# Batch norm behind a matmul: another form and place for the fourth tile's normalisation, denser column chunks, later outputs of the fifth tile

## Chip, cores, metric

One core of a Trainium2 chip. The metric is the device time of one execution in microseconds (us). A run of this one-core kernel counts as slow when it is over 1.5% above the fastest of the same kernel; ratios use the other runs.

## The reference

```python
batch, m, k, n = 16, 512, 1024, 768
y = np.matmul(x, weight)                       # (16, 512, 768), M = 8192 rows
mean = np.mean(y, axis=(0, 1), keepdims=True)
var = np.var(y, axis=(0, 1), keepdims=True)
return (gamma * (y - mean) / np.sqrt(var + eps) + beta).astype(np.float32)
```

The statistics go over all rows, so no output can be stored before its column's last matmul.

## The kernel before

The 768 columns are six tiles of 128. The first three are computed while x is loaded, then their statistics are closed, and their outputs leave as *row products* (VectorE multiplies, L283; GpSimd adds the shift, L289) or, for 4 of the 16 chunks of 512 rows, as *column chunks* (normalise, transpose on TensorE, copy on ScalarE, store). Meanwhile TensorE computes the fourth, fifth and sixth tile. Their outputs leave in *pairs* of chunks: two normalisations, eight transposes, one copy of 1.0 us, one store of 512 KB. The sixth tile's go singly at the end, 16 stores of 256 KB. A schedule written in model times (`at(t, ...)`) is sorted and fixes each engine's order.

```python
def norm(nt, c, eng):
    if eng == "act":
        seq(nc.scalar.activation(y(nt, c), y(nt, c), AF.Identity,
            bias=shift[:, nt:nt + 1], scale=scale[:, nt:nt + 1]))
    else:
        seq((nc.vector if eng == "dve" else nc.gpsimd).tensor_scalar(
            y(nt, c), y(nt, c), scale[:, nt:nt + 1], shift[:, nt:nt + 1],
            op0=ALU.mult, op1=ALU.add))
# ... cut ...
def outputs(nt, t0, step):
    for b in range(C // 2):                    # pairs of chunks
        tb = t0 + step * b
        if nt == NT - 2 and b >= C // 2 - HELD:
            held.append(b)                     # the fifth tile's last pair waits for the end
            continue
        for i in range(2):
            at(tb - 2.2 + 0.5 * i, norm, nt, 2 * b + i, "act" if tb < tr + 2.0 and i == 0 else "dve")
        at(tb, turn_y, (nt,), 2 * b * CH, 2 * RT)
        at(tb + 2.2, out_copy, (nt,), 2 * b * CH, "act")
        at(tb + 2.3, store, (nt,), 2 * b * CH, 2 * RT)
# ... cut: the matmuls of tiles 3 to 5; pe is the model time at which a tile's matmuls end ...
    if nt == GA:
        outputs(nt, S + 37.0, 2.3)             # fourth tile
    elif nt < NT - 1:
        outputs(nt, pe + 4.6, 1.85)            # fifth tile
    else:
        held_outputs(nt - 1, pe)
        last_outputs(nt, pe + 3.0)             # sixth tile
```

The transposes stand between the matmuls, one after each, until they run out. A transpose that waits for its normalisation holds up all matmuls behind it.

## Time and profile before

| | before |
|---|---|
| time | 219.95 us, median of 3 (219.61 to 220.23); 219.41 over 6 runs later |
| span of the profiled run | 217.6 us |
| busy: TensorE, VectorE, ScalarE, GpSimd | 92%, 72%, 56%, 62% |
| first store | 136 us |

The span is read as four terms that add up: the start of the column sums (L232, when the loading stage is over; it scatters by up to 2 us between profiles), from there to the first half-chunk matmul (L330, the sixth tile's last chunk), from there to the last DMA byte, and a rest. I call the second the *matmul phase* and the third the *tail*. TensorE's timeline of the kernel before has the two marks:

```profile
123.21 1.39 PE L232 MATMUL tot_ps<-ones,sum 128*128 128x1 f32 x12
197.38 1.98 PE L330 MATMUL y_ps<-xT_sb,w_sb 128*128 128x256 bf16 x16
```

The last DMA byte is worked out from stretches of 2 us: in the last one that moved data, its GB/s over 346, the rate of a full DMA here, tell how far into it the transfer reached. Before: matmul phase 74.2, tail 18.6 (197.4 to 216.0).

### The profile page before, as it was taken

How to read it: one execution, taken by the hardware profiler on the slowest of the kernel's cores; microseconds unless marked ns; L12 is line 12 of the kernel's file. 1: busy time of each engine (PE TensorE's matmuls, PEld its weight loads, DVE VectorE, ACT ScalarE, POOL GpSimd, SP SyncE). 2: the span in 40 equal slices, each digit the busy share in tenths (PEclk: the TensorE clock that was granted, in tenths of full speed). 3: DMA queues.
4: the chain of work that ended last, by engine and by line, in shares of the span. 5: the costliest groups of instructions: out<-in, count | busy, mean ns of one | idle time of the engine just before them, and what ended most of it. 6: DMA issues, size and time to landing. Idle time of an engine off the chain costs nothing.

```text
span 217.6 us, 3451 instructions
## 1 busy us (share of the span) xinstructions
PE 200.3 (92%) x1178; PEld 104.9 (48%) x1178; DVE 155.8 (72%) x263; ACT 121.2 (56%) x227; POOL 134.2 (62%) x153
## 2 busy tenths in 40 slices
PE   7997999999999999999999999999999979997900
PEld 2452555554544565645656545444444435554600
DVE  3222978887978789998654369988899999728900
ACT  2001463645543466645666414967866689976950
POOL 8887686878684699953558304999995963000000
PEclk9999999999999999999999999999999999999985
DMA  5999999999999999993000000897877989999998
GB/s 70 156 196 187 191 196 196 197 197 196 196 189 195 197 196 196 196 197 49 0 5 0 0 0 0 305 348 293 304 286 293 332 274 370 338 347 284 282 345 243
DMA packets 70161, 43.75 MB, mean 201 GB/s; under 512 B 4096, under 2 KB 69632, under 8 KB 70144
## 3 DMA queue, kind: packets, MB, share of 16 engines
q0 software_dynamic: 34624, 18.36, 61.6%
q1 hardware_dynamic: 35520, 25.18, 35.8%
q8 instruction: 9, 0.15, 0.3%
q14 instruction: 8, 0.07, 0.1%
HBM read 36.71 MB, written 25.17 MB: 284 GB/s over the span
## 4 chain that ended last, share of the span: by engine, by line
PE 75%; DVE 8%; DMA 5%; POOL 3%; issue 3%; ACT 2%; ACTq 1%; POOLq 0%
PE y_ps L196 39%; PE y_ps L186 29%; PE o_ps L398 5%; DMA w_sb<-in_weight_dram 3%; DMA ring<-in_x_dram 2%; DVE stats L316 2%; DVE y_sb L382 2%; DVE ring L283 2%; POOL w_sb L149 2%; DVE o_sb L283 1%; ACT o_sb L411 1%; POOL ring L162 1%; PE y_ps L330 1%; PE a_ps L272 1%; PE tot_ps L232 1%
## 5 line engine op out<-in xcount | busy, mean ns | idle before, releaser
L196 PE MATMUL y_ps<-xT_sb,w_sb 128*128 128x512 bf16 (+1 forms) x484 | 117.6, 381 | 1.6 <-DMA w_sb<-in_weight_dram 1.3
L196 PEld LDWEIGHTS <-w_sb 128*128 128x128 bf16 x484 | 45.9, 96 | 59.3 <-issue 3.1
L343 ACT CAST y_sb<-y_ps 128x512 bf16<-128x512 f32 x59 | 34.5, 585 | 53.7 <-DVE stats L316 50.7
L186 PE MATMUL y_ps<-w_sb,xT_sb 128*128 128x384 bf16 x384 | 63.4, 326 | 0.0
L316 DVE BATCH_NORM_STATS2 stats<-y_ps 128x6 f32<-128x512 f32 x58 | 39.3, 685 | 19.9 <-PE y_ps L196 19.9
L162 POOL DMA_DIRECT2D ring<-in_x_dram x72 | 45.2, 633 | 11.9 <-DVE xT_sb L174 6.5
L186 PEld LDWEIGHTS <-xT_sb 128*128 128x128 bf16 x384 | 37.5, 98 | 25.6
L212 POOL TENSOR_TENSOR sum<-sum,sq_sb 128x384 f32<-128x384 f32 x38 | 38.0, 1001 | 18.4 <-ACT sq_sb L208 17.1
L174 DVE STREAM_TRANSPOSE xT_sb<-ring 128x1024 f32<-128x1024 f32 (+1 forms) x34 | 39.5, 1168 | 12.8 <-DMA ring<-in_x_dram 12.8
L398 PE MATMUL o_ps<-ident,y_sb 128*128 128x128 bf16 x240 | 38.2, 219 | 3.6 <-DVE y_sb L382 2.5
L289 POOL TENSOR_TENSOR ring<-ring,sum 128x768 f32<-128x768 f32 x17 | 31.1, 1864 | 13.1 <-ACT sum L274 12.1
L215 DVE TENSOR_TENSOR sum<-y_ps,sum 128x384 f32<-128x384 f32 x48 | 26.1, 544 | 14.4 <-ACT sq_sb L208 13.4
L208 ACT ACTIVATE sq_sb<-y_ps 128x384 f32<-128x384 f32 x48 | 23.4, 492 | 15.2 <-PE y_ps L186 11.6
L221 ACT CAST y_sb<-y_ps 128x384 bf16<-128x384 f32 x48 | 22.9, 476 | 7.3 <-DVE sum L215 7.0
L411 ACT CAST ring<-o_ps 128x1024 f32<-128x1024 bf16 (+1 forms) x24 | 22.5, 951 | 4.2 <-PE o_ps L398 2.7
L398 PEld LDWEIGHTS <-y_sb 128*128 128x128 bf16 x240 | 19.4, 97 | 8.6 <-DVE y_sb L382 3.3
L382 DVE TENSOR_SCALAR y_sb<-y_sb,scale,shift 128x512 bf16<-128x512 bf16 x43 | 22.0, 565 | 0.0
L283 DVE TENSOR_TENSOR ring<-y_sb,a_ps 128x768 f32<-128x768 bf16 x17 | 15.9, 937 | 0.0
L289 POOL TENSOR_TENSOR o_sb<-o_sb,sum 128x768 f32<-128x768 f32 x7 | 13.2, 1880 | 2.9 <-DVE o_sb L283 2.9
L377 ACT ACTIVATE y_sb<-y_sb,shift,scale 128x512 bf16<-128x512 bf16 x17 | 13.5, 816 | 0.0
L155 PE MATMUL idle_ps<-idle_sb 128*128 128x512 bf16 x38 | 11.0, 456 | 1.2 <-DVE idle_sb L103 1.2
L411 ACT CAST o_sb<-o_ps 128x512 f32<-128x512 bf16 x16 | 7.9, 679 | 0.3 <-PE o_ps L398 0.3
(62 smaller groups left out, 50.1 us busy)
## 6 DMA issues: line engine op xcount, KB each, us to landing
ring<-in_x_dram POOLq DMA_DIRECT2D x56, 256.0 KB, 8.6
out_dram<-ring SPq DMA_DIRECT2D x25, 384.0 KB, 3.0
out_dram<-ring SPq DMA_DIRECT2D x16, 512.0 KB, 5.1
out_dram<-o_sb SPq DMA_DIRECT2D x16, 256.0 KB, 3.7
out_dram<-o_sb SPq DMA_DIRECT2D x7, 384.0 KB, 3.4
ring<-in_x_dram POOLq DMA_DIRECT2D x16, 128.0 KB, 5.3
w_sb<-in_weight_dram POOLq DMA_DIRECT2D x8, 96.0 KB, 4.6
w_sb<-in_weight_dram POOLq DMA_DIRECT2D x4, 192.0 KB, 5.6
```

Source lines behind the costliest of these rows:

```text
L162: seq(nc.gpsimd.dma_start(x_bf[32 * i:32 * i + 32], src[:, :, KQ * i:KQ * (i + 1)]))
L174: seq(nc.vector.transpose(dst[:, half, :, jw0:jw1], src[:, :, jw0:jw1]))
L186: seq(nc.tensor.matmul(y_ps, xT[c][:, jw, s * P:(s + 1) * P, e], w_sb[:, jw, e, 0:NA], start=(jw == 0 and e == 0), stop=(jw == JW - 1 and ...
L196: seq(nc.tensor.matmul(y_ps, w_sb[:, jw, e, nt * P:(nt + 1) * P], xT[c][:, jw, q0 * QR:q1 * QR, e], start=(jw == 0 and e == 0 and q0 == 0) ...
L212: seq(eng.tensor_add(acc, acc, py.pop(("sq", c, s))))
L215: seq(nc.vector.tensor_add(sum1, py["row", c, s][:, 0:NA], sum1))
L289: seq(nc.gpsimd.tensor_add(o_sb, o_sb, sum1[:, None, :].to_broadcast([P, 2, NA])))
L316: seq(nc.vector.bn_stats(stats_of(nt)[:, i, :], py[nt, c]))
L343: seq(nc.scalar.copy(y(nt, c), py.pop((nt, c))))
L382: seq((nc.vector if eng == "dve" else nc.gpsimd).tensor_scalar(y(nt, c), y(nt, c), scale[:, nt:nt + 1], shift[:, nt:nt + 1], op0=ALU.mult, ...
L398: seq(nc.tensor.transpose(dst, src, ident))
L411: seq(nc.scalar.copy(o_sb, src))
```

## The change

Its aim, as far as its words and code tell: keep VectorE from waiting for GpSimd. The fourth tile's VectorE normalisations get a form without a fast mode, more of them go to ScalarE, pairs come less often, and the fifth tile's start after the crowd.

```diff
+        elif eng == "dve1":
+            seq(nc.vector.scalar_tensor_tensor(
+                y(nt, c), y(nt, c), scale[:, nt:nt + 1],
+                shift[:, nt:nt + 1].to_broadcast([P, CH]), op0=ALU.mult, op1=ALU.add,
+            ))
@@ column chunks
-            tk += 9.6 if c else 7.2
+            tk += 8.2 if c else 7.2
@@ outputs()
-                at(tb - 2.2 + 0.5 * i, norm, nt, 2 * b + i, "act" if tb < tr + 2.0 and i == 0 else "dve")
+                at(tb - (2.8 if tb < tr else 2.2) + 0.5 * i, norm, nt, 2 * b + i,
+                   "dve" if tb > tr + 2.0 else "dve1" if i and b % 2 == 0 else "act")
@@ starts and steps
-            outputs(nt, S + 37.0, 2.3)
+            outputs(nt, S + 36.0, 2.8)
-            outputs(nt, pe + 4.6, 1.85)
+            outputs(nt, pe + 10.5, 2.3)
```

## The prediction

> **What bounds the kernel now.** I read the page first: the 40 slices, then the chain that ended last.
>
> ```profile
> PE   7997999999999999999999999999999979997900
> DVE  3222978887978789998654369988899999728900
> DMA  5999999999999999993000000897877989999998
> PE 75%; DVE 8%; DMA 5%; POOL 3%; issue 3%; ACT 2%; ACTq 1%; POOLq 0%
> ```
>
> TensorE is busy to slice 37; the output DMA is full in the last ten slices or so. The chain in order of time says where TensorE is not the bound: it runs on TensorE from 19.3 to 156.9 us, on VectorE to about 178.7 us, on TensorE again to 199.4 us (the last statistics), then through the last tile's outputs to the end. So two stretches matter: 157 to 179 us, and the tail. VectorE's timeline in the first:
>
> ```profile
> 161.26 3.38 DVE L382 TENSOR_SCALAR y_sb<-y_sb,scale,shift 128x512 bf16<-128x512 bf16 x1
> 166.03 1.62 DVE L382 TENSOR_SCALAR y_sb<-y_sb,scale,shift 128x512 bf16<-128x512 bf16 x1
> 173.80 0.45 DVE L382 TENSOR_SCALAR y_sb<-y_sb,scale,shift 128x512 bf16<-128x512 bf16 x1
> ```
>
> The same form has a median of 0.41 us over its 43 calls. GpSimd's timeline explains the excess:
>
> ```profile
> 160.86 1.84 POOL L289 TENSOR_TENSOR o_sb<-o_sb,sum 128x768 f32<-128x768 f32 x1
> 162.65 1.84 POOL L289 TENSOR_TENSOR ring<-ring,sum 128x768 f32<-128x768 f32 x1
> 165.67 1.83 POOL L289 TENSOR_TENSOR o_sb<-o_sb,sum 128x768 f32<-128x768 f32 x1 [1.18 <-DVE o_sb L283]
> 172.22 1.88 POOL L289 TENSOR_TENSOR ring<-ring,sum 128x768 f32<-128x768 f32 x1
> ```
>
> Each normalisation ends 0.15 us after a GpSimd addition ends (164.64 after 164.49, 167.65 after 167.50, 174.25 after 174.10). The first waited out two additions, because the second was already ready when it asked; the others waited only for the running one. What reaches TensorE of this is small:
>
> ```profile
> 167.71 0.23 PE L398 MATMUL o_ps<-ident,y_sb 128*128 128x128 bf16 x1 [0.30 <-DVE y_sb L382]
> 170.64 0.23 PE L398 MATMUL o_ps<-ident,y_sb 128*128 128x128 bf16 x1 [0.50 <-DVE y_sb L382]
> 175.32 0.23 PE L398 MATMUL o_ps<-ident,y_sb 128*128 128x128 bf16 x1 [0.23 <-ACT y_sb L377]
> 178.69 0.23 PE L398 MATMUL o_ps<-ident,y_sb 128*128 128x128 bf16 x1 [0.94 <-ACT y_sb L377]
> ```
>
> From start to start, beside the usual 0.28 us, these four lose 0.41, 0.61, 0.34 and 1.05: 2.4 us. That is all that can be won there. The tail, in stretches of 2 us (the last two columns are the DMA's share and GB/s):
>
> ```profile
> 198.00:200.00 2.00, 1.80 (x20) 1.43 (x18) 1.30 (x4) 0.96 (x2) 0.00 (x0) 1.00 1.15 343
> 200.00:202.00 2.00, 0.53 (x8) 0.44 (x8) 1.73 (x9) 1.57 (x4) 0.00 (x0) 1.00 0.20 59
> 202.00:204.00 2.00, 2.00 (x28) 1.37 (x25) 2.00 (x8) 2.00 (x5) 0.00 (x0) 1.00 0.96 292
> 204.00:206.00 2.00, 2.00 (x28) 1.37 (x26) 2.00 (x7) 2.00 (x5) 0.00 (x0) 1.00 1.15 347
> ```
>
> The DMA has emptied its queue at about 200.2, idles 2 us, starts again at about 202.3 and then runs at 346 GB/s to 216.0: one held store of 512 KB and sixteen of 256 KB, 4.72 MB, 13.6 us. The end of the span is 1.6 us later. Before the gap the fifth tile's stores have kept it full since 186.
>
> **What the Trainium skill says.** (1) "SBUF — State Buffer", section "SBUF: two separate sides": VectorE and GpSimd share one pair of ports, as an exclusive lock for a whole instruction; a VectorE operation takes it in a two-port mode or with two SBUF inputs (then only against a GpSimd operation that reads SBUF). The waits above agree for the two-port mode. For two inputs the earlier stage has two cases, L212, an addition of two SBUF tensors that normally takes 0.55 us:
>
> ```profile
> 89.43 0.77 DVE L212 TENSOR_TENSOR sum<-sum,sq_sb 128x384 f32<-128x384 f32 x1
> 94.81 1.10 DVE L212 TENSOR_TENSOR sum<-sum,sq_sb 128x384 f32<-128x384 f32 x1
> ```
>
> GpSimd's triples that started at 86.62 and 92.32 end at 89.79 and 95.50; these two end at 90.20 and 95.91, both 0.41 us later. They waited too. (2) "VectorE: DVE Perf Modes", section "The perf-mode tier table": `tensor_scalar` in bf16 reaches four elements a cycle, a two-tensor operation with an fp32 operand one. The trace agrees: 0.41 us for 512 elements above, 0.55 us for 384 in L212.
>
> **The change, part by part.**
> (a) *Fourth tile.* Before: nine normalisations in the fast form on VectorE, seven on ScalarE. The built order of the changed kernel has nine on ScalarE, three of the new form (the second chunk of pairs 0, 2 and 4), four fast ones for pairs 6 and 7 (a pair is two chunks that are stored together). The new form reads y and a broadcast fp32 shift, two SBUF inputs. Free, I estimate 0.68 us: L283's 768 elements take 0.94, L212's 384 take 0.55, so 512 lie at 0.68. So it is 0.27 us dearer, and if it locks, it waits like the old one and ends 0.54 us after GpSimd, not 0.15.
> (b) *Working it through with the lock*, with the durations above, in the new order: the first one asks at 159.8, waits for the running addition and a ready one, to 162.7, and ends at 163.2. The second asks at 167.7, gets in at 169.65, ends at 170.2. The third asks at 174.0, ends at 175.3. Behind it stand the last statistics (0.69), a row product (0.94) and the aggregate (0.57), so the aggregate is done at 177.3, against 176.2 before. ScalarE then has, in order, the square root, a cast, three small affine steps, a copy of 1.0 and only then pair 5's first normalisation: 180.3. TensorE wants it at 177.7. Stalls: 0.2 for pair 1, 0.6 for pair 2 (ScalarE behind casts that wait for VectorE), 0.1, then 2.6 and 0.1: 3.6 us in place of 2.4.
> (c) *Fifth tile later.* The order of TensorE's instructions shows 72 transposes behind the last matmul before, 92 after: 20 fewer in the matmul stream. There a transpose adds 0.056 us (0.282 against 0.226 a step), so the last matmul comes 1.1 us sooner. The 20 fit into TensorE's idle 2 us while the last statistics are finished.
> (d) *The tail.* Those 20 belong to half of pair 4 and to pairs 5 and 6, so three stores of 512 KB move behind the last matmul, 1.5 us of DMA each. Pair 4's copy on ScalarE cannot start until its last four transposes, 0.35 us after the last matmul (199.4 in the old times); copy 1.0; 0.95 from its end until the DMA flows, as with the held store before: 201.7. From there 4 x 512 KB + 16 x 256 KB = 6.29 MB at 346 GB/s are 18.2 us, ending at 219.9 against 216.0: **+3.9 us**, less what the last matmul is earlier. The DMA's spare time meanwhile lies at 187 to 200, where stores of 1.5 us come every 2.3 us.
> (e) *Denser column chunks* bring twelve transposes ahead of the VectorE-bound stretch and change no count.
> Sum: +3.9 (d), -1.1 (c), +1.2 (b) = +4.0 with the lock, so about 224; without the lock and without stalls, 3.9 - 1.1 - 2.4 = +0.4, so 220.3.
>
> **The rivals.**
> *Plain mode is free of the lock.* Then VectorE takes back some 6 us and all stalls go: 220.3. For it: the change seems made with that in mind, and the second operand has step zero, which no run here has tried. Against: the two L212 cases and the skill's page.
> *TensorE's gain passes whole to the end*, the tail being hidden: 2.4 + 1.1 us won, 216.5. Against: the tail has 18.2 us of transfer behind one copy that comes after the last matmul; the order of the instructions fixes that. I see no way round it.
> *The stalls grow*: ScalarE, in order, carries two more normalisations and waits on VectorE in between; one more wait for a ready addition (1.84 us) makes 226.
>
> **Range and chances.** The tail's +3.9 I hold for firm within 0.5; the stalls are uncertain by 1.5 us, as I may have a request on the wrong side of a GpSimd addition, and slips more often loosen than tighten this sum. I give the lock 70%. That puts the middle at 222.6, between 220.3 and 224. Slower by over 2% needs 224.35, which the lock case reaches in a fifth to a quarter of its outcomes: 0.15. Faster by 2% needs 215.6, below even the rival with everything won: 0.02.
>
> **What would show it.** Lock: the three new operations last 1.4 to 3.5 us each and end about 0.54 after a GpSimd addition; at 0.7 they are free of it. Stalls: TensorE's waits at its transposes in 160 to 181 us add up to over 2 us and the largest is on ScalarE near 178; under 1 us proves (b) wrong. Tail: DMA share below 0.9 between 187 and 199, full for about 18 us at the end, and last matmul to last DMA byte 20.5 us instead of 16.6. If the last distance stays at 17, (d) is wrong; then I am too high by 3 us.

## The result

222.38 us (median of 6, 221.34 to 223.07) against 219.41 (6 runs): ratio 1.0133, 95% interval 1.0089 to 1.0177, which is "same" at 2%; the interval lies above 1, so the changed kernel is slower, by 0.9 to 1.8%. The span of the profiled run is 220.6 us. The page of the changed kernel, the same rows as shown of before:

```profile
PE   7997999999999999999999999999999979997400
DVE  3222878887978789998554289988999995588300
DMA  5999999999999999990000001996995999888997
PE 71%; DMA 9%; DVE 8%; ACT 5%; issue 2%; POOL 1%; ACTq 0%; POOLq 0%
```

In the 40 slices the DMA row is the one to look at: before, its last nine slices read 989999998, now 999888997, and the chain has 9% of DMA instead of 5%. TensorE's marks:

```profile
123.45 1.39 PE L232 MATMUL tot_ps<-ones,sum 128*128 128x1 f32 x12
196.23 1.98 PE L330 MATMUL y_ps<-xT_sb,w_sb 128*128 128x256 bf16 x16
```

The matmul phase is 72.8, **1.4 us shorter** than before. Yet the end is later. The tail in stretches of 2 us (last two columns: DMA share, GB/s), first the last stretch of the kernel before, then the changed kernel:

```profile
214.00:216.00 2.00, 0.00 (x0) 0.00 (x0) 0.00 (x0) 0.00 (x0) 0.00 (x0) 0.50 1.13 339
```

```profile
188.00:190.00 2.00, 2.00 (x22) 1.22 (x20) 0.64 (x2) 1.89 (x3) 0.00 (x0) 1.00 0.32 96
196.00:198.00 2.00, 2.00 (x20) 1.61 (x18) 1.97 (x7) 1.44 (x3) 0.00 (x0) 1.00 0.72 217
198.00:200.00 2.00, 1.77 (x30) 1.58 (x28) 1.16 (x5) 1.49 (x4) 0.00 (x0) 1.00 0.53 157
200.00:202.00 2.00, 0.98 (x13) 0.69 (x14) 1.91 (x8) 2.00 (x4) 0.00 (x0) 1.00 0.85 254
218.00:220.00 2.00, 0.00 (x0) 0.00 (x0) 0.00 (x0) 0.00 (x0) 0.00 (x0) 0.50 0.42 125
```

The DMA idles where it was full before (345 GB/s at 188, 348 at 196) and is full from about 200.5 on to 218.7 (218 + 2 x 125/346; before, 214 + 2 x 339/346 = 216.0). The tail is 22.5 us instead of 18.6: **+3.9**. With +0.2 for the start of the column sums and +0.3 for the rest behind the last byte, +0.2 - 1.4 + 3.9 + 0.3 = +3.0, the difference of the two spans.

The new form on VectorE:

```profile
160.03 3.46 DVE L383 SCALAR_TENSOR_TENSOR y_sb<-y_sb,scale,shift 128x512 bf16<-128x512 bf16 x1
167.81 0.80 DVE L383 SCALAR_TENSOR_TENSOR y_sb<-y_sb,scale,shift 128x512 bf16<-128x512 bf16 x1
172.32 2.10 DVE L383 SCALAR_TENSOR_TENSOR y_sb<-y_sb,scale,shift 128x512 bf16<-128x512 bf16 x1
```

and GpSimd's additions beside it:

```profile
161.09 1.85 POOL L289 TENSOR_TENSOR o_sb<-o_sb,sum 128x768 f32<-128x768 f32 x1
...
166.22 1.83 POOL L289 TENSOR_TENSOR o_sb<-o_sb,sum 128x768 f32<-128x768 f32 x1
168.02 2.27 POOL L289 TENSOR_TENSOR ring<-ring,sum 128x768 f32<-128x768 f32 x1
...
173.84 2.27 POOL L289 TENSOR_TENSOR o_sb<-o_sb,sum 128x768 f32<-128x768 f32 x1
```

All three end 0.55 us after an addition ends (163.49 after 162.94, 168.61 after 168.05, 174.42 after 173.87): they wait like the fast form did. Where VectorE went first, the next addition lasts 2.27 instead of 1.83, so GpSimd waits too. TensorE's waits at its transposes:

```profile
169.15 0.23 PE L404 MATMUL o_ps<-ident,y_sb 128*128 128x128 bf16 x1 [0.37 <-ACT y_sb L377]
179.50 0.23 PE L404 MATMUL o_ps<-ident,y_sb 128*128 128x128 bf16 x1 [1.63 <-ACT y_sb L377]
```

Two stalls, 2.0 us of idle time, as much as the four before. The larger is the predicted one: pair 5's first normalisation on ScalarE, behind the aggregate and what ScalarE does with it.

### The profile page after: what moved, and what is told of

It is laid out like the page before. It is cut to its first block, busy times and chain, and to the rows that moved or that the text cites. A ratio compares the mean times of both kernels' runs of the same rounds, so it can differ in the third digit from the quotient of the medians.

```text
span 220.6 us, 3437 instructions
## 1 busy us (share of the span) xinstructions
PE 199.3 (90%) x1163; PEld 105.2 (48%) x1178; DVE 154.9 (70%) x262; ACT 121.2 (55%) x228; POOL 134.7 (61%) x153
## 4 chain that ended last, share of the span: by engine, by line
PE 71%; DMA 9%; DVE 8%; ACT 5%; issue 2%; POOL 1%; ACTq 0%; POOLq 0%
PE y_ps L196 38%; PE y_ps L186 28%; DMA ring<-in_x_dram 4%; PE o_ps L404 3%; DMA w_sb<-in_weight_dram 3%; DVE y_sb L383 3%; DVE stats L316 2%; ACT o_sb L417 2%; DVE ring L283 2%; DMA out_dram<-o_sb 2%; ACT ring L417 2%; DVE o_sb L283 1%; POOL ring L162 1%; PE y_ps L330 1%; PE a_ps L272 1%
## 5 line engine op out<-in xcount | busy, mean ns | idle before, releaser
L196 PE MATMUL y_ps<-xT_sb,w_sb 128*128 128x512 bf16 (+1 forms) x470 | 115.2, 381 | 2.6 <-DMA w_sb<-in_weight_dram 1.4
L316 DVE BATCH_NORM_STATS2 stats<-y_ps 128x6 f32<-128x512 f32 x58 | 39.3, 686 | 20.8 <-PE y_ps L196 20.5
L404 PE MATMUL o_ps<-ident,y_sb 128*128 128x128 bf16 x240 | 37.6, 218 | 4.2 <-ACT y_sb L377 2.0
L388 DVE TENSOR_SCALAR y_sb<-y_sb,scale,shift 128x512 bf16<-128x512 bf16 x39 | 14.6, 437 | 0.0
L377 ACT ACTIVATE y_sb<-y_sb,shift,scale 128x512 bf16<-128x512 bf16 x18 | 14.4, 823 | 0.0
L417 ACT CAST o_sb<-o_ps 128x512 f32<-128x512 bf16 x16 | 8.5, 678 | 0.6 <-DMA out_dram<-o_sb 0.5
```

Of the source, the lines that this page charges most:

```text
L196: seq(nc.tensor.matmul(y_ps, w_sb[:, jw, e, nt * P:(nt + 1) * P], xT[c][:, jw, q0 * QR:q1 * QR, e], start=(jw == 0 and e == 0 and q0 == 0) ...
L316: seq(nc.vector.bn_stats(stats_of(nt)[:, i, :], py[nt, c]))
L404: seq(nc.tensor.transpose(dst, src, ident))
L417: seq(nc.scalar.copy(o_sb, src))
```

## The experiments

The table has, from each run's profile, TensorE's idle time before transposes up to 192 us, the matmul phase and the tail; the number of transposes behind the last matmul ("behind") is read from the built program, and the twelve traces show the same numbers. Each run has one profile. All outputs are right.

| run | time, us | ratio to before (95%) | behind | idle | phase | tail |
|---|---|---|---|---|---|---|
| before | 219.41 | 1 | 72 | 2.0 | 74.2 | 18.6 |
| changed | 222.38 | 1.013 (1.009 to 1.018) | 92 | 2.0 | 72.8 | 22.5 |
| e1 fourth tile only | 219.58 | 0.998 (0.994 to 1.002) | 72 | 1.9 | 73.9 | 18.6 |
| e2 fifth later only | 222.90 | 1.016 (1.011 to 1.020) | 92 | 2.3 | 73.5 | 22.5 |
| e3 changed, fifth as before | 218.87 | 0.997 (0.994 to 0.999) | 72 | 1.1 | 72.8 | 18.6 |
| e4 changed, shift in PSUM | 219.18 | 0.999 (0.995 to 1.004) | 92 | 0 | 70.4 | 22.5 |
| e5 denser columns only | 219.46 | 1.000 (0.996 to 1.004) | 72 | 1.9 | 74.1 | 18.6 |
| e6 = e3 + e4 | 216.96 | 0.989 (0.986 to 0.992) | 72 | 0 | 71.5 | 18.6 |
| e7 changed, fifth halfway | 219.94 | 1.002 (0.998 to 1.005) | 72 | 2.0 | 73.7 | 18.9 |
| e8 changed, 80 behind | 220.60 | 1.006 (1.003 to 1.010) | 80 | 2.0 | 73.2 | 20.3 |
| e9 before, PSUM form | 216.86 | 0.983 (0.980 to 0.987) | 72 | 0 | 71.5 | 18.6 |
| e10 before, SBUF form | 221.18 | 1.003 (0.999 to 1.008) | 72 | 3.9 | 76.2 | 18.6 |

The kernel before took 219.4 to 220.4 us (medians) beside them; the ratios allow for that. One run of e1 (221.96) counts as slow and is left out of its ratio.

**Theory:** the loss is the fifth tile's move, through what then stands behind the last matmul. **Rival:** it is the fourth tile's new form and fuller ScalarE. e1 to e3 separate them.

**e1: the fourth tile's part alone.**

```diff
-            tk += 8.2 if c else 7.2
+            tk += 9.6 if c else 7.2
-            outputs(nt, pe + 10.5, 2.3)
+            outputs(nt, pe + 4.6, 1.85)
```

(against the changed kernel). 

> The kernel before with the fourth tile's part of the change alone (nine chunks on ScalarE, three in the new form, start at 36.0, step 2.8). Theory (the loss is in the tail, and 72 transposes stay behind the last matmul here): 0 to +0.5 us against before, the distance from the first half-chunk matmul to the last DMA byte 18.6 us as before; new form 0.8 to 3.5 us each, because of the port lock. Rival (the locked new form and the fuller ScalarE cost the 3 us): +2 to +3 us with the tail's distance unchanged.

Measured: no difference from before, tail 18.6, the new form 3.47, 0.79 and 2.05 us. With this placement the rule also gives it one chunk of the fifth tile's first pair, which met no addition: 0.74 us. The rival, +2 to +3 us, falls.

**e2: the fifth tile later, alone.**

```diff
-            outputs(nt, pe + 4.6, 1.85)
+            outputs(nt, pe + 10.5, 2.3)
```

> The kernel before with the fifth tile's outputs later, alone (10.5 and 2.3). Theory: 92 transposes behind the last matmul, the distance from the first half-chunk matmul to the last DMA byte 22.5 us in place of 18.6, last matmul about 1.1 us earlier: +2.5 to +3.2 us. Rival (the fourth tile is to blame): within 0.7 us of before.

Measured: ratio 1.016, tail 22.5. This line alone costs what the whole change costs. The matmul phase is only 0.6 shorter, not 1.1, as there is a fifth stall of 0.3 us.

**e3: the changed kernel with the fifth tile put back** (the reverse edit). 

> The changed kernel with the fifth tile's outputs put back (4.6 and 1.85). Theory: the 3 us come back, -0.5 to +0.5 us against before, with the tail's distance 18.6. Rival (fourth tile): stays at +2 to +3.

Measured: 218.87, tail 18.6, slightly faster than before. The idle time is 1.1 instead of 2.0, though VectorE's and GpSimd's orders are the same until 177 us. The first new operation explains it; VectorE, then GpSimd in this run:

```profile
160.31 1.64 DVE L383 SCALAR_TENSOR_TENSOR y_sb<-y_sb,scale,shift 128x512 bf16<-128x512 bf16 x1
```

```profile
159.56 1.83 POOL L289 TENSOR_TENSOR ring<-ring,sum 128x768 f32<-128x768 f32 x1
161.36 2.29 POOL L289 TENSOR_TENSOR o_sb<-o_sb,sum 128x768 f32<-128x768 f32 x1
```

It asks 0.75 us after the running addition's start, as in the changed kernel (0.73, 160.03 after 159.30), with the next addition ready in both; here VectorE goes next, there GpSimd did. So part of e3's gain is who went first. These two profiles do not tell why, but all together they sort. In eight runs there are 13 such requests where the next addition had had its input for 0.5 us when VectorE asked: in the seven asked 0.40 to 0.74 us after the running addition's start GpSimd went next, in the six asked at 0.75 to 1.59 us VectorE did. e3's first stands on that edge. One more, in e5, was asked at 0.88, the addition's input ready for 1.0 us, and GpSimd went next. No run varied the moment of asking on purpose, so this is an order seen, not a cause shown.

**e4: the second operand from PSUM.** VectorE reads the shift from a spare column of the bank that holds the row products' scale, so that the form has one SBUF input.

```diff
+            aff["bank"] = a_ps                 # in spread_rows(0)
-                shift[:, nt:nt + 1].to_broadcast([P, CH]), op0=ALU.mult, op1=ALU.add,
+                aff["bank"][:, NA:NA + 1].to_broadcast([P, CH]), op0=ALU.mult, op1=ALU.add,
+        if nt == GA:                           # in finish_affine: the shift once more, into PSUM
+            seq(nc.scalar.activation(aff["bank"][:, NA:NA + 1], mv[:, nt, 0:1], AF.Identity,
+                bias=beta_sb[:, one], scale=nscale))
```

> The changed kernel, with the new form's broadcast operand read from a spare column of a PSUM bank, so that it has one SBUF input. Lock theory: the three new operations last 0.65 to 0.75 us whatever GpSimd does, where they took 3.46, 0.80 and 2.10; the fourth tile's last statistics come 3 to 4 us of VectorE time sooner, TensorE's stalls fall from 2.2 to under 1 us, and the time is 1 to 2 us below the changed kernel's, thus still above before's. Rival (GpSimd delays any VectorE operation that reads or writes SBUF): the three still last up to 3.5 us and the time stays.

Measured: VectorE, and GpSimd's additions beside the first,

```profile
159.20 0.73 DVE L389 SCALAR_TENSOR_TENSOR y_sb<-y_sb,scale,a_ps 128x512 bf16<-128x512 bf16 x1
165.15 0.73 DVE L389 SCALAR_TENSOR_TENSOR y_sb<-y_sb,scale,a_ps 128x512 bf16<-128x512 bf16 x1
170.28 0.74 DVE L389 SCALAR_TENSOR_TENSOR y_sb<-y_sb,scale,a_ps 128x512 bf16<-128x512 bf16 x1
```

```profile
158.48 1.83 POOL L291 TENSOR_TENSOR ring<-ring,sum 128x768 f32<-128x768 f32 x1
160.28 1.82 POOL L291 TENSOR_TENSOR o_sb<-o_sb,sum 128x768 f32<-128x768 f32 x1
```

0.73 us from 159.20, in the midst of an addition (158.48 to 160.31) that is not lengthened either. TensorE has no stall left. The gain on the changed kernel, 1.4% or about 3 us by the ratios, is more than the 1 to 2 expected: the matmul phase gave 2.4, and the rest is within what the intervals leave open. The tail is still 22.5, so the end is only level with before.

**e5: denser column chunks alone** (the `tk` line on the kernel before). 

> The kernel before with the denser column chunks alone (step 8.2). Theory: counts unchanged, tail's distance 18.6 us, same stalls: within 0.5 us of before. Rival (denser chunks collide with the row products on ScalarE or VectorE): +0.5 us or more, with new stalls between 145 and 160 us.

Measured: 1.000, the same four stalls. This part shows no effect by itself.

**e6: both repairs** (e4's edit and the fifth tile put back). 

> The changed kernel with both repairs: the new form's second operand in PSUM and the fifth tile's outputs as before. Theory: no long stalls, tail's distance 18.6 us; the first half-chunk matmul comes 71.5 us after the column sums (74.2 before, 72.8 in the changed kernel), so 1.5 to 2.5 us under before, 217.2 to 218.2 us, and the fastest of all. Rival (the store queue, full since 186 us, then sets the end instead): no better than the version with the fifth tile alone put back, 218.9.

Measured: 1.1% under before; 216.96 is 0.2 below the range given, phase 71.5 as expected. The rival, 218.9, falls.

**e7: fifth tile halfway,** `outputs(nt, pe + 7.5, 2.0)` in the changed kernel: later, but still 72 behind. 

> The changed kernel with the fifth tile's outputs started at 7.5 with step 2.0: 3 us later than before and wider, but still 72 transposes behind the last matmul. Theory (what stands behind the last matmul counts, not lateness): tail's distance 18.6 to 19 us, time within 0.6 us of the version with the fifth tile put back (218.9). Rival (lateness itself starves the store queue): about half the loss, 220.5.

Measured: tail 18.9, so lateness hardly costs anything there. The time alone would not decide: 219.94 lies between the theory's and the rival's. It misses the 0.6 us I had allowed by 0.5, since I compared it with e3, which had the luck described above: e7's idle time is the changed kernel's 2.0, and its phase 0.9 longer than e3's.

**e8: eight more behind,** `outputs(nt, pe + 8.5, 2.1)`. 

> The changed kernel with the fifth tile's outputs at 8.5 with step 2.1: 80 transposes behind the last matmul, eight more than before, one store of 512 KB more. Theory: tail's distance 18.6 + 1.5 = 20.1 us, last matmul 0.45 us earlier: about +1 us on the version with 72, 219.5 to 220.5. Rival (the loss comes at the full 20 only, from the copy of the split pair in front of the square root): as with 72, 218.9.

Measured: tail 20.3, one store of 512 KB (1.5 us) more than 18.6, and 220.60, just above the range. With e7 and the changed kernel the tail follows the count: 72, 80, 92 give 18.6 to 18.9, 20.3, 22.5. In e7 and e8 four transposes stand between the two half-chunks, 0.2 us that the tail includes; from the last matmul's end to the last byte it is 16.6 before, 16.7 in e7, 18.1 in e8 and 20.5 in the changed kernel. The rival falls.

**e9 and e10: the form alone, on the kernel before.** The seven VectorE normalisations of the fourth tile that stand among row products get the new form; nothing is moved. In e9 the second operand is in PSUM, in e10 in SBUF.

```diff
-                at(tb - 2.2 + 0.5 * i, norm, nt, 2 * b + i, "act" if tb < tr + 2.0 and i == 0 else "dve")
+                at(tb - 2.2 + 0.5 * i, norm, nt, 2 * b + i,
+                   "dve" if tb > tr + 2.0 else "act" if i == 0 else "dve1" if nt == GA else "dve")
```

> The kernel before with its seven VectorE normalisations of the fourth tile that stand among the row products in the two-operand form, second operand in PSUM, and nothing else of the change. Lock theory: each lasts 0.73 us; TensorE's stalls (2.4 us before) fall under 1 us, the first half-chunk matmul comes 72 to 73 us after the column sums in place of 74.2, tail's distance 18.6: 1.2 to 2.2 us below before. Rival (the wider spread and fuller ScalarE of the change are needed as well): within 0.7 us of before.

> The same with the second operand in SBUF, as the change has it. Lock theory: the seven wait for GpSimd as the fast form did and end 0.54 us after an addition, so -0.3 to +1.5 us against before. Rival (the form without a fast mode is what spares the wait): as the run with the operand in PSUM.

Measured: e9 is by its ratio the fastest kernel, 1.7% under before (216.86 beside 220.40; e6's interval touches it), its idle time 0. That is more than the 1.2 to 2.2 us expected, 3.7 by the ratio. The phase, 71.5, lies below the range too and gives 2.6 of it; the spans of the two profiled runs differ by 2.8. The kernel before took 1.0 us more in these rounds than in its profiled run (219.41), and nothing tells why. Its first three, then those of e10:

```profile
161.10 0.73 DVE L389 SCALAR_TENSOR_TENSOR y_sb<-y_sb,scale,a_ps 128x512 bf16<-128x512 bf16 x1
163.34 0.73 DVE L389 SCALAR_TENSOR_TENSOR y_sb<-y_sb,scale,a_ps 128x512 bf16<-128x512 bf16 x1
166.32 0.74 DVE L389 SCALAR_TENSOR_TENSOR y_sb<-y_sb,scale,a_ps 128x512 bf16<-128x512 bf16 x1
```

```profile
160.51 3.77 DVE L383 SCALAR_TENSOR_TENSOR y_sb<-y_sb,scale,shift 128x512 bf16<-128x512 bf16 x1
165.68 2.01 DVE L383 SCALAR_TENSOR_TENSOR y_sb<-y_sb,scale,shift 128x512 bf16<-128x512 bf16 x1
169.93 1.07 DVE L383 SCALAR_TENSOR_TENSOR y_sb<-y_sb,scale,shift 128x512 bf16<-128x512 bf16 x1
```

e10 idles 3.9 us and its phase is 2.0 longer than before, though its time, 1.003 (0.999 to 1.008), is not shown to differ; the expectation of -0.3 to +1.5 us holds. e9 and e10 differ in where one operand lies (and in the small ScalarE operation that puts it there): 4.6 us of matmul phase, and 4.3 us in the medians. So the lack of a fast mode alone spares no wait (e10), and one SBUF tensor input alone does not either, for the fast form has no more than that and waited in the kernel before. The two together do (e4, e6, e9).

## Why the prediction was right

The time, 222.38, is close to the 222.6 predicted and the class is as predicted. By its steps:

- **(d), the tail, +3.9:** right as worked out: 22.5 against 18.6, and e2, e4, e7 and e8 show that it follows the number of transposes behind the last matmul, and with them of stores, and not the fourth tile or lateness. The distance from the last matmul to the last byte was to be 20.5; it is 20.5 (218.7 less 198.2, where the line of L330 ends). A sign named with it came only in part: the DMA share was to stay below 0.9 from 187 to 199, and was 1.09 and 1.15 from 190 to 194.
- **(c), 20 transposes fewer in the stream, -1.1:** right. The cleanest pair is e4 and e6, both without stalls, 20 apart: 70.4 against 71.5.
- **(a), the lock:** right. The new form ends 0.55 after an addition where 0.54 was estimated, and takes 0.73 to 0.75 alone where 0.68 was. The rival "plain mode is free of the lock" is refuted by the change itself and by e10.
- **(b), stalls of 3.6 us: too large.** From start to start the two stalls lose 0.5 and 1.7, 2.2 in all. (Both this and the prediction's 2.4 count from the start of the matmul before and take off 0.28, which is the step from transpose to transpose; from matmul to transpose it is 0.22. Put right, the kernel before loses 2.6 and the changed one 2.3, and -1.1 - 0.3 is the -1.4 of the matmul phase.) The failed term is the second new operation's wait: I had it ask at 167.7 and get in at 169.65, behind an addition that was ready first; it asked at 167.81 and got in at 168.05. The rule I took from the kernel before, that a ready addition goes first, does not hold: here the addition had its input from 167.28, and e3 shows the first request decided the other way. What stood behind it came 0.8 to 0.9 us sooner: the aggregate was done at 176.4 instead of 177.3, pair 5's first normalisation at 179.5 instead of 180.3.
- **(e), no change of count:** right, by e5.

So the lock branch by itself said +4.0, where the spans have +3.0: the matmul phase came out 1.5 better than its +0.1, and the start of the column sums and the rest at the end, which it did not foresee, 0.5 worse. The middle of 222.6 came from giving the refuted branch 30%, and from a hunch that slips rather loosen the sum than tighten it. That the number is so close is luck in that part: these misses work against each other. What was sound is the mechanism of the tail.

What stays open: why, when an addition and a VectorE operation both wait, one or the other goes next, and whether the order by the moment of asking (e3) is a rule; and whether e3's gain of 0.4% would hold over many profiles.

## What to carry to other kernels

Count what the instruction order leaves behind the last matmul: where the store queue is full from there to the end, stores moved there lengthen the tail, here by 1.5 us for one of 512 KB and 3.9 for three. A VectorE operation that collided with GpSimd was freed here by a form without a fast mode that also takes its second tensor input from PSUM; that one edit on the kernel before won 1.7%, while the same form with both inputs in SBUF cost TensorE another 2 us in its profile. Where a change bundles several moves, split the span into terms that add up and undo them one by one: here one line cost the whole 3.9 us of tail, and the rest of the change by itself moved the time by 0.4% or less (e1, e3).

## What the Trainium skill lacked or had wrong

- "SBUF — State Buffer", section "SBUF: two separate sides", states the lock for two SBUF inputs, and the runs agree. It does not say that a [128, 1] operand broadcast with step zero counts as one: it does (0.8 to 3.8 us in the changed kernel and e10, against 0.73 with that operand in PSUM).
- The same section says who holds the pair, not who is next when both sides wait. Both outcomes occur, 3.46 us in the changed kernel and 1.64 in e3 for the same request, asked 0.73 and 0.75 us after the running addition's start.
- "VectorE: DVE Perf Modes", section "The perf-mode tier table", has no row for this two-operand form with a per-partition scale: 0.73 us for 512 bf16 elements with an fp32 second operand, against 0.41 for the fast form alone.
